# The last block's LayerNorm, split between two phases of a convolution and RWKV-7 block

## The chip, the cores and the metric

The kernel runs on one core of one Trainium2 chip. The metric is the device time of one execution in microseconds (us); several runs are given, with their median. The profile is of one further execution.

## The reference

One decoder block for 2048 tokens of width 1024, in float32. One input projection feeds two branches; both end in a projection of their own, are merged by gates, go through an output projection and are added to the residual. A final RMSNorm closes it.

```python
def _conv_branch(val, gate, og, conv_k, conv_b, ln_g, ln_b, w_o):
    u = val * jax.nn.sigmoid(gate)
    u = _causal_depthwise_conv(u, conv_k, conv_b)      # width 31
    u = _layernorm(u, ln_g, ln_b, LN_EPS)              # over the 1024 channels
    u = jax.nn.silu(u) * jax.nn.silu(og)
    return u @ w_o
```

The other branch is RWKV-7 time mixing: r, k, v, a decay and a learning rate from low-rank (LORA) projections, a delta-rule recurrence over 16 heads, a norm per head, times a gate, times `w_o` of its own. In short: x is normed and modulated, projected to all of these; out = RMSNorm(x + gate · (merged branches @ `w_out`)).

## The kernel before

**Tiling.** Channels lie on the 128 partitions, so 1024 channels are 8 tiles, and the tokens go in 4 blocks `b` of 512: a tile is 128x512, 256 KB. A projection of one output tile (`project`) is 24 matmuls of 128x128 by 128x512: 8 input tiles, each three times, since a float32 is split into a high and a low part (hi·hi, lo·hi, hi·lo). The weights' two parts are made once, stored (`kh_in`, `kl_in`, `kh_ro`, `kl_ro`, `kh_o`, `kl_o`) and loaded as `w_hi` and `w_lo`; `presplit` makes them for the two out projections, as side work.

**Phase 1** runs over the blocks, and in a block over four groups `g` of four heads. A group is one call of `slot`: it emits the projections of its two pairs of heads (k, r, vv each) and between them "fill" projections (convolution gate and value, and four gates). `order(b, g)` lists them: after the first pair's three come `FIRST` = 5 fills, after the second pair's the rest. At the head of a block but the first stands the LORA projection; the input tiles of the next block are loaded as `hf` and split to `h_hi` and `h_lo` when four items of the last slot are left (`rest == 4`); in the last block those are the tiles of `z_d` of block 0, which phase 2's first projections need, and which phase 1 already emits at its end.

Everything else is written as generators (`pair`, `group`, `taps`, `lnorm_first`, `sides`, ...), which a planner polls while the program is written. Each step waits until the planner's own count of time says that its operands, buffers or an engine are free, and is emitted there. So the order on each engine is fixed when the program is written, and on the chip an instruction waits only for semaphores. All of SP's DMA issues stand in one queue. Shared 128x512 buffers are handed out by a ring `hx` of `HXB` = 7. The four `As` buffers of two groups and the two `uv` buffers are allocated in `opened` at the head of a slot, which waits until the group before the last has been normed.

A group's path: `pair` loads `wf` (its slice of the LORA weights), makes `wl`, `As` matrices and so on; `group` inverts the small triangular systems with transfers through DRAM (`dA`, `La`, `dT`, back to `As`), transposes `Tn`, goes over the chunks, and stores the normed outputs times gate (`zb`, `zr` loaded, `z_d` stored).

**Convolution and its LayerNorm.** `taps` makes a tile by 31 operations on DVE and stores it in `y_d`. `lnorm_first(b)` has three passes over the 8 tiles. Pass 1 loads and sums them (7 additions), and a matmul with ones gives the mean. Pass 2 loads again, subtracts, squares and sums; a matmul and a few steps give `rl`, the reciprocal standard deviation. Pass 3 loads again, and per tile: times `rl`, tanh and affine form on ACT, (tanh + 1) times it, times the gate tile from `co_d`, stored in `u_d`. For blocks 0 to 2 this runs on POOL one block later. For block 3 it runs on DVE at the end of phase 1 (`last_norm`), with buffers from `more`, to which `lend(3)` lends three of `hx`.

**Phase 2** is written per block without the planner, and a scheduler orders it: `cproj` (for b > 0), then `pout` (x + merged @ `w_out`, four column blocks of 96 matmuls 128x256), `addx`, the final RMSNorm `finish` (8 DVE operations `xt<-xt,rs,fg`, 8 stores `out<-xt`), and `rproj(b + 1)`. The loads `zt<-z_d` and `zt<-u_d` (`lsplit`) feed these with 8 buffers `ld`. Two facts matter here. The tiles `xt{n}` (residual rows) and `mr{n}` (merged sums of the next block) share a buffer, tag `mr{n}`, so `rproj`'s first write of `mr` waits for the store `out<-xt` of the same n. And its PSUM tiles `ps_main` have two buffers.

The profile gives line 132 for every operation, since a helper records them all; operations are told apart by their names, without numbers.

Of the kernel before, what the change touches and what calls it, by code (L numbers as in the profile page):

```python
# [9 lines left out]
F32 = mybir.dt.float32  # L10
# [34 lines left out]
LDB = 8  # L45
SLACK = 2.0
KEPT = ("in",)
FILL = ("c", "1", "3", "4", "2", "c", "1", "3", "4", "2")
LAST = ("c0 10 20 c1 21 11 22 c2 23", "c3 12 24 c4 25 13 26 c5 27", "c6 14 30 c7 31 15 32 33 34 35",
        "16 36 37 40 41 17 42 43 44 45 46 47")  # L50
DMA_RATE = 330e3
FIRST = 5
AHEAD = 0.7
BANKS = {"aux": 2, "late": 1, "xo": 2}
# [20 lines left out]
def hybrid_block(ctx: ExitStack, tc: tile.TileContext, x, vecs, convk, w2a2, final_g, ada, w_in, w_co, w_ro, w_o, crow, out,  # L75
# [199 lines left out]

    u_dram = scratch("u_d")

    grow_d = dp.tile([D], F32, name="grow_d", tag="grow_d")
# [243 lines left out]

    hx = Ring(HXB, hx0)
    t2r = Ring(T2B, lambda name: e2.tile([P, TB], F32, name=name, tag="t2", bufs=T2B))
    wr = Ring(WB, lambda name: whl.tile([P, KT, P], F32R, name=name, tag="w", bufs=WB))
# [251 lines left out]
    def pair(G, q_, box):  # L777
        b, pr, uv, Asb = G.b, 2 * G.g + q_, G.uv, G.As[q_]
        wf = e1.tile([P, 2, P], F32, name="wf", tag="wf")
# [35 lines left out]
        k = box["k"]  # L815
        yield ok(k)
        KR = l3.tile([P, NCH // 2, 4 * CH], F32, name="KR", tag="KR", bufs=KRB)
        BK = l3.tile([P, NCH // 2, 4 * CH], F32, name="BK", tag="BK", bufs=BKB)
# [73 lines left out]
        nc.scalar.copy(rk, pb)  # L892
        yield when(lambda: "v" in box)
        vv = box["v"]
# [13 lines left out]
    def opened(b, g, h, lora):  # L908
        G = Group()
        G.b, G.g, G.h, G.lora, G.tri, G.pairs, G.chained, G.gated, G.normed = b, g, h, lora, 0, 0, False, False, False  # L910
        G.uv = l3.tile([P, NCH, 2, P], F32, name="uv", tag="uv", bufs=2)
        G.dN = dp.tile([2, 2, NCH // 2, 2, 2, 32], F32, name="dN", tag="dN", bufs=3)
        G.As = [l3.tile([P, 2, NCH, P], F32, name="As", tag="As", bufs=ASB) for _ in range(2)]
        G.R = [{}, {}]
        return G
# [4 lines left out]
    def group(G, before):  # L920
        g, b, As, uv, R = G.g, G.b, G.As, G.uv, G.R
        yield when(lambda: G.tri == 2)
# [4 lines left out]
        for q in range(2):  # L927
            for e in range(2):
                p0 = 64 - 64 * e
                for bk in range(2):  # L930
                    sl = slice(p0 + 32 * bk, p0 + 32 * bk + 32)
                    nc.sync.dma_start(dA[q, :, :, e, bk].rearrange("h c s t -> s (h c) t"), heads(As[q])[sl, e::2, sl])
        La = lt.tile([P, 32, 32], F32, name="La", tag="La", bufs=1)
        dAl = dA.rearrange("q h c e k s t -> (q h c e k) s t")
# [31 lines left out]
        for q in range(2):  # L966
            for e in range(2):
# [4 lines left out]
                yield idle("SP", 0.1)  # L972
        yield when(lambda: G.pairs == 2 and (before is None or before.chained))
        yield ok(*As)

# [78 lines left out]
        locked[0] = False  # L1054
        O = uv[:, 0::2]
# [133 lines left out]

    convs = []  # L1190

    def taps(b, j, u, before):
        if before is not None:
            yield when(lambda: before.done)
        yield ok(u)
        yj = e2.tile([P, TB], F32, name="yj", tag="yj", bufs=1)
        acc = pc.tile([P, TB], F32, name="acc", tag="acc")
        nc.vector.tensor_scalar(out=acc, in0=u[:, HALO:], scalar1=ck[:, j, HALO:HALO + 1], scalar2=vc("conv_b", j),
                                op0=ALU.mult, op1=ALU.add)
        for i in range(HALO):  # L1200
            yield idle("DVE", AHEAD)
            nc.vector.scalar_tensor_tensor(out=acc if i + 1 < HALO else yj, in0=u[:, i:i + TB],
                                           scalar=ck[:, j, i:i + 1], in1=acc, op0=ALU.mult, op1=ALU.add)
        yield ok(yj)
        nc.sync.dma_start(y_dram[b][j], yj)
# [4 lines left out]

    def lnorm_first(b, hx):

# [7 lines left out]
        eng = nc.vector if b + 1 == NB else nc.gpsimd  # L1220
        yield hx.room(3, 1)
        ys, nxt = yload(0), yload(1)
        for j in range(1, KT):
            yj = nxt
            if j + 1 < KT:
                yield hx.room(1, 1)
                nxt = yload(j + 1)
            yield ok(ys, yj)
            eng.tensor_tensor(out=ys, in0=ys, in1=yj, op=ALU.add)
            hx.give(yj)  # L1230
        yield burst(ok(ys), free, bank("late"))
# [33 lines left out]
        hx.give(qs, rt, mean)  # L1265
        def both_of(j):
            yj, ct = yload(j), hx.take("lnc")
            nc.sync.dma_start(ct, co_dram[b][j])
            return yj, ct

        nxt = None
        for j in range(KT):
            if nxt is None:
                yield hx.room(3, 1)
                nxt = both_of(j)
            else:
                yield hx.room(1)
            yj, ct = nxt
            th, nxt = hx.take("lnth"), None
            if j + 1 < KT and b + 1 == NB and hx.room(2)() is not None:  # L1280
                nxt = both_of(j + 1)
            yield ok(yj, rl)
# [79 lines left out]
    def sides(b, g):  # L1362
        if b + 1 < NB:
            yield from xnorm(b + 1, XN[g])
            if g == 1:
                normed[0] = b + 1
        if b == 1 and g == 0:
            yield from gate_col()
        if b and g == (0 if b + 1 == NB else 1):
            yield from lnorm_first(b - 1, hx)  # L1370
            if b + 1 == NB:
                yield from lend(3)
        if b:
            for _ in range(0 if b + 1 == NB else (1, 1, 3, 3)[g]):
                n_ = later.pop(0)
                for half in range(2):
                    yield from presplit(*n_, half)
# [19 lines left out]
    def last_norm():  # L1397
        yield when(lambda: len(convs) == KT * NB and convs[-1].done)
        yield from lnorm_first(NB - 1, more)

# [13 lines left out]
    def order(b, g):  # L1414
# [11 lines left out]
        for q in range(2):  # L1426
            for name, t_ in (("k", T_K), ("r", T_R), ("vv", T_V)):
                yield name, q, t_ + 2 * g + q
            yield from fill(FIRST if q == 0 else len(todo))

# [15 lines left out]
    def slot(b, g, h, lora, new):  # L1446
        until(lambda: not Gs[:-1] or Gs[-2].normed)
        G = opened(b, g, h, lora)
# [123 lines left out]
    def lsplit(src, hl=None):  # L1572
# [3 lines left out]
        return hi, lo  # L1576

    def cproj(b, uhl, mhl):
        for n in range(KT):
# [40 lines left out]
    for b in range(NB):  # L1620
# [115 lines left out]
```

## Time and profile before

| | |
|---|---|
| three runs | 2885.52, 2889.28, 2889.45 us; median 2889.28 us |
| the profiled execution | 2893.26 us, its span 2891.5 us |
| TensorE's mean granted clock | 0.984 |
| TensorE (PE) busy | 2722.4 us, 94% |
| VectorE (DVE) busy | 2067.5 us, 72% |
| ScalarE (ACT) busy | 1092.9 us, 38% |
| GpSimd (POOL) busy | 1195.6 us, 41% |
| phase 1 ends at about | 2420 us |

A row of the timeline gives start, duration, engine, operation, output and inputs; a bracket behind it gives how long the engine had stood idle and what ended that. "SPq" is a DMA issue on SP's queue: its duration is that of issuing, not of the transfer. In the chain of waits each piece is released by the piece above it. In the table by stage a number in brackets counts instructions, and the granted clock is a share of full speed.

### The profile page before, as it was taken

To read this page: it belongs to the slowest core of one execution; us is meant where nothing else is said; L and a number is where in the kernel's file an instruction comes from. 1 tells how busy PE (TensorE), PEld (TensorE's weight loads), DVE (VectorE), ACT (ScalarE), POOL (GpSimd) and SP (SyncE) were. 2 spreads that over 40 slices of the span, in tenths; PEclk is the share of its full clock that TensorE was granted. 3 is DMA by queue.
4 is the path that set the end of the run, shared out by engine and by line. 5 is a ranking of instruction groups with operands and counts; after the bars stand their busy time and mean duration, and the time that the engine had idled before them with its cause. 6 is when DMAs were issued, how large, how long until landed. Compare 5 with 4: busy or idle time off the path is not lost. (4 is left out here: it accounts for less than half of the span.)

```text
span 2891.5 us, 52406 instructions
## 1 busy us (share of the span) xinstructions
PE 2722.4 (94%) x19472; PEld 2195.2 (76%) x19472; DVE 2067.5 (72%) x3598; ACT 1092.9 (38%) x2181; POOL 1195.6 (41%) x1725
## 2 busy tenths in 40 slices
PE   6999999989999999999999998999999998999998
PEld 5777777767777777777777776877777777898988
DVE  6877887869677878886878786888887576343343
ACT  5545444434243434443434343324343334121211
POOL 1564746533528364534564553474543612000000
PEclk9999999989999999999999999999999999999999
DMA  8776867666758677767666776676665778777664
GB/s 329 258 286 206 292 218 265 236 233 228 235 185 290 199 255 242 275 222 238 231 251 223 249 255 197 220 269 215 227 230 191 273 247 315 259 239 247 215 226 175
DMA packets 370959, 697.26 MB, mean 241 GB/s; under 512 B 135184, under 2 KB 153936, under 8 KB 370704
## 3 DMA queue, kind: packets, MB, share of 16 engines
q1 hardware_dynamic: 370704, 693.91, 70.3%
q8 instruction: 154, 2.52, 0.4%
q14 instruction: 101, 0.83, 0.1%
HBM read 500.63 MB, written 192.02 MB: 240 GB/s over the span
## 5 line engine op out<-in xcount | busy, mean ns | idle before, releaser
L132 PE MATMUL ps_main<-h_hi,w_hi 128*128 128x512 f32 x2432 | 1016.3, 418 | 16.7 <-DVE lora L132 4.6
L132 PE MATMUL ps_main<-h_hi,w_lo 128*128 128x512 f32 x2432 | 966.9, 398 | 25.3 <-POOL w_lo L132 14.6
L132 PE MATMUL ps_main<-h_lo,w_hi 128*128 128x512 f32 x2432 | 961.3, 395 | 0.5 <-DVE h_lo L132 0.5
L132 DVE SCALAR_TENSOR_TENSOR acc<-u,ck,acc 128x512 f32<-128x512 f32 x928 | 698.0, 752 | 27.9 <-POOL u L132 2.2
L132 PEld LDWEIGHTS ps_main<-h_hi,w_lo 128*128 128x128 f32 x2432 | 462.2, 190 | 140.1 <-POOL w_lo L132 18.7
L132 PEld LDWEIGHTS ps_main<-h_hi,w_hi 128*128 128x128 f32 x2432 | 463.3, 190 | 128.4 <-issue 13.3
L132 PEld LDWEIGHTS ps_main<-h_lo,w_hi 128*128 128x128 f32 x2432 | 463.7, 191 | 96.3 <-issue 8.7
L132 POOL TENSOR_TENSOR w_lo<-w_st,w_hi 128x1024 fp32r<-128x1024 f32 (+1 forms) x82 | 165.0, 2012 | 332.5 <-ACT w_hi L132 288.5
L132 ACT ACTIVATE th<-ps_main 128x512 f32<-128x512 f32 x160 | 95.5, 597 | 360.2 <-PE ps_main L132 311.5
L132 POOL TENSOR_TENSOR TT<-TT,itmp 128x126 f32<-128x126 f32 (+22 forms) x496 | 209.5, 422 | 38.9
L132 POOL TENSOR_TENSOR itmp<-La,TT 128x126 f32<-128x126 f32 (+22 forms) x496 | 203.5, 410 | 37.7 <-issue 7.9
L132 ACT CAST w_hi<-w_st 128x1024 fp32r<-128x1024 f32 (+1 forms) x135 | 127.4, 945 | 221.6 <-DMA w_st<-w_co_t 78.4
L132 DVE SCALAR_TENSOR_TENSOR S<-xo,pe,Se 64x64 f32<-64x64 f32 x512 | 145.0, 283 | 91.9 <-PE xo L132 69.4
L132 ACT COPY uv<-xo 64x256 f32<-64x256 f32 (+1 forms) x192 | 81.2, 439 | 251.3 <-PE xo L132 184.7
L132 DVE TENSOR_TENSOR w_lo<-w_st,w_hi 128x1024 fp32r<-128x1024 f32 x53 | 74.5, 1405 | 68.3 <-PE ps_main L132 51.6
L132 DVE TENSOR_TENSOR As<-aux,maskA 128x512 f32<-128x512 f32 x128 | 82.3, 685 | 49.0 <-PE aux L132 48.9
L132 ACT ACTIVATE Se<-S,pe 128x128 f32<-128x128 f32 x256 | 89.0, 397 | 67.2 <-DVE S L132 66.7
L132 PEld LDWEIGHTS aux<-KR,BK 64*128 64x128 f32 x1024 | 66.3, 191 | 44.3 <-POOL KR L132 21.1
L132 PE MATMUL aux<-KR,BK 64*128 64x128 f32 x1024 | 80.0, 290 | 20.7 <-POOL KR L132 14.0
L132 POOL TENSOR_TENSOR wlo<-wf,wl 64x128 fp32r<-64x128 f32 x64 | 31.3, 489 | 159.2 <-ACT wl L132 156.7
L132 DVE TENSOR_TENSOR xt<-pout,xt 128x256 f32<-128x256 f32 x64 | 24.4, 420 | 100.1 <-PE pout L132 100.1
L132 PEld LDWEIGHTS xo<-S,KR 128*128 128x128 f32 x512 | 77.1, 189 | 20.7 <-ACT Se L132 4.3
(283 smaller groups left out, 5005.4 us busy)
## 6 DMA issues: line engine op xcount, KB each, us to landing
w_hi<-kh_in SPq DMA_DIRECT2D x219, 512.0 KB
w_lo<-kl_in SPq DMA_DIRECT2D x219, 512.0 KB
w_st<-w_in_t SPq DMA_DIRECT2D x73, 512.0 KB
kh_in<-w_hi SPq DMA_DIRECT2D x71, 512.0 KB
kl_in<-w_lo SPq DMA_DIRECT2D x71, 512.0 KB
lny<-y_d SPq DMA_DIRECT2D x96, 256.0 KB
w_hi<-kh_ro SPq DMA_DIRECT2D x32, 512.0 KB
w_lo<-kl_ro SPq DMA_DIRECT2D x32, 512.0 KB
```

Of the source, the lines that this page charges most:

```text
L132: r = f(*a, **k)
```

## The change

1. Block 3's y tiles are summed by `taps` as each is finished, in an `hx` buffer `ysum`; `lnorm_first` takes the sum and leaves pass 1 out. Behind `rl` it stores `rl` to DRAM (`rl_d`) and ends. Pass 3 is done in phase 2, by `ulast`, which takes the place of `lsplit(u_dram[3])`: 17 loads (`rl`, eight `yt`, eight `ct`) instead of eight, three DVE and two ACT operations a tile ahead of the split.
2. The weight splits of `presplit` in blocks 1, 2, 3 go by `LATE_W`, 6, 6 and 4, where before 8 and 8 stood in blocks 1 and 2 and none in 3. `LEND` is 1 instead of 3. Pass 3 of blocks 0 to 2 loses its early loads (they were for block 3 alone).
3. `As` is taken in `pair`, when the group before the last has been chained, `uv` when it has been normed; the wait at the head of `slot` goes. `group` waits for `before.merged` ahead of its `La` load.
4. In the last group of block 3 the second pair's projections come after 1 fill instead of 5 (`FIRST_LAST`), and the loads of `z_d` of block 0 begin when 9 items are left, not 4 (`HLAST`).

```diff
+LEND = 1
+LATE_W = ((), (1, 1, 2, 2), (1, 1, 2, 2), (1, 1, 1, 1))
+FIRST_LAST = 1
+HLAST = 9
...
     def pair(G, q_, box):
-        b, pr, uv, Asb = G.b, 2 * G.g + q_, G.uv, G.As[q_]
+        b, pr = G.b, 2 * G.g + q_
...
+        yield when(lambda: G.prior is None or G.prior.chained)
+        Asb = l3.tile([P, 2, NCH, P], F32, name="As", tag="As", bufs=ASB)
+        G.As.append(Asb)
...
-        yield when(lambda: "v" in box)
+        yield when(lambda: "v" in box and (G.prior is None or G.prior.normed))
+        if q_ == 0:
+            G.uv = l3.tile([P, NCH, 2, P], F32, name="uv", tag="uv", bufs=2)
...
     def group(G, before):
+        yield when(lambda: before is None or before.merged)
         La = lt.tile([P, 32, 32], F32, name="La", tag="La", bufs=1)
...
     def taps(b, j, u, before):
+        if b + 1 == NB and j == 0:
+            yield hx.room(1)
+            ysum.append(hx.take("ysum"))
+            nc.scalar.copy(ysum[0], yj)
+        elif b + 1 == NB:
+            yield ok(ysum[0], yj)
+            nc.vector.tensor_tensor(out=ysum[0], in0=ysum[0], in1=yj, op=ALU.add)
...
-    def lnorm_first(b, hx):
+    def lnorm_first(b, hx, ys=None):
...
+        if b + 1 == NB:
+            yield ok(rl)
+            nc.sync.dma_start(rl_d, rl)
+            hx.give(rl)
+            return
...
-                yield from lend(3)
+                yield from lend(LEND)
...
-            for _ in range(0 if b + 1 == NB else (1, 1, 3, 3)[g]):
+            for _ in range(LATE_W[b][g]):
...
-            yield from fill(FIRST if q == 0 else len(todo))
+            yield from fill(len(todo) if q else FIRST_LAST if (b, g) == (NB - 1, 3) else FIRST)
...
     def slot(b, g, h, lora, new):
-        until(lambda: not Gs[:-1] or Gs[-2].normed)
...
-            if new is not None and rest == 4:
+            if new is not None and rest == (4 if b + 1 < NB else HLAST):
...
+    def ulast(hl):
+        rl = f2.tile([P, TB], F32, name="rl", tag="rl", bufs=1)
+        nc.sync.dma_start(rl, rl_d)
+        for j in range(KT):
+            yt, ct = ldt("yt", y_dram[NB - 1][j]), ldt("ct", co_dram[NB - 1][j])
+            th = ob.tile([P, TB], F32, name="uth", tag="uth")
+            nc.vector.tensor_tensor(out=yt, in0=yt, in1=rl, op=ALU.mult)
+            nc.scalar.activation(th, yt, AF.Tanh, scale=hlg[:, j:j + 1], bias=hlb[:, j:j + 1])
+            nc.scalar.activation(yt, yt, AF.Identity, scale=vc("conv_ln_g", j), bias=vc("conv_ln_b", j))
+            nc.vector.scalar_tensor_tensor(out=yt, in0=th, scalar=1.0, in1=yt, op0=ALU.add, op1=ALU.mult)
+            nc.vector.tensor_tensor(out=yt, in0=yt, in1=ct, op=ALU.mult)
+            split(hl[0][j], hl[1][j], yt, nc.vector)
+        return hl
...
-            uhl = lsplit(u_dram[b + 1], utiles())
+            uhl = lsplit(u_dram[b + 1], utiles()) if b + 2 < NB else ulast(utiles())
```

The first place at which the order changes is DVE's, in phase 2, between the output projection of block 1 and `rproj` of block 2 (`m_lo` is the split of block 3's z tiles, `vs`, `rs` and `rs_t` are the small steps of the final RMSNorm, `xt<-xt,rs,fg` its first big one). Before, from the last residual addition on:

```order
L132 TENSOR_TENSOR xt_26727<-pout,xt_26727 128x256
L132 TENSOR_TENSOR m_lo_27920<-zt,m_hi_27912 128x512
L132 TENSOR_TENSOR m_lo_27921<-zt,m_hi_27913 128x512
L132 TENSOR_TENSOR m_lo_27922<-zt,m_hi_27914 128x512
L132 TENSOR_REDUCE vs<-sq_26777 128x4
L132 TENSOR_SCALAR vs<-vs 128x4
```

Ten further small steps follow, and then the first `xt<-xt,rs,fg`. After, at the end of the same stretch of DVE's order, behind seven operations of the new third pass (`yt`) that stand between the last residual addition and these rows:

```order
L136 SCALAR_TENSOR_TENSOR yt_28356<-uth_28360,yt_28356 128x512
L136 SCALAR_TENSOR_TENSOR rs_t_27188<-rs_t_27188,vs_27184 128x4
L136 TENSOR_TENSOR yt_28356<-yt_28356,ct_28358 128x512
L136 SCALAR_TENSOR_TENSOR rs2_27187<-rs_t_27188,rs2_27187 128x4
L136 SCALAR_TENSOR_TENSOR yt_28368<-uth_28372,yt_28368 128x512
L136 TENSOR_TENSOR rs_t_27188<-rs2_27187 128x4
L136 TENSOR_TENSOR yt_28368<-yt_28368,ct_28370 128x512
L136 SCALAR_TENSOR_TENSOR rs_t_27188<-rs_t_27188,vs_27184 128x4
L136 TENSOR_TENSOR yt_28380<-yt_28380,rl_28330 128x512
L136 SCALAR_TENSOR_TENSOR rs2_27187<-rs_t_27188,rs2_27187 128x4
L136 SCALAR_TENSOR_TENSOR xt0_26613<-xt0_26613,rs2_27187,fg_25433 128x512
```

In all 13 `yt` operations stand ahead of the first `xt<-xt,rs,fg` that stood behind it before, one of them ahead of the last residual addition; the last is the multiplication of the fifth tile, `yt_28380`. SP's order at the same place, after:

```order
L136 DMA w_hi_27321<-kh_ro3_11786 128x1024
L136 DMA w_lo_27322<-kl_ro3_11787 128x1024
L136 DMA yt_28380<-y_d3_4_191 128x512
L136 DMA ct_28382<-co_d3_4_223 128x512
L136 DMA yt_28392<-y_d3_5_192 128x512
L136 DMA w_hi_27353<-kh_ro4_11981 128x1024
L136 DMA w_lo_27354<-kl_ro4_11982 128x1024
L136 DMA ct_28394<-co_d3_5_224 128x512
L136 DMA out<-xt0_26613 128x512
```

The load of the fifth y tile stands behind the weights of `ro` tile 3, and the weights of tile 4 now stand ahead of the stores `out`; before, six of these stores stood between the weights of tiles 3 and 4.

The second place is SP's queue at the end of block 2 (`hf<-xT3` are block 3's input tiles, `gc_d2_7` is the last gate of block 2, `zb` and `zr` are loaded for a pair's outputs). Before, all eight `hf` loads stand ahead of the weights `kh_in48`, some of the last of the block. After, three do, and the rest stand here:

```order
L136 DMA gc_d2_7_250<-th_18302 128x512
L136 DMA zb_18333<-bv_d2_4_119 128x512
L136 DMA zr_18334<-ro_d2_4_151 128x512
L136 DMA hf_18346<-xT3_66 128x512
L136 DMA hf_18359<-xT3_66 128x512
L136 DMA kh_o1_0_17936<-w_hi_18120 128x512
L136 DMA hf_18372<-xT3_66 128x512
L136 DMA kl_o1_0_17937<-w_lo_18121 128x512
L136 DMA hf_18392<-xT3_66 128x512
L136 DMA hf_18394<-xT3_66 128x512
```

They moved behind the last store of block 2 and among a `presplit`'s stores (`kh_o`, `kl_o`). At the start of block 2, `wf` of the first pair now stands ahead of four of the eight `As` loads that stood ahead of it before; and at the end of block 3, five of the eight loads of `z_d` of block 0 stand well ahead, where before four did.

More of the change, by code (lines that the diff above doesn't have):

```diff
@@ L276, in hybrid_block @@
     u_dram = scratch("u_d")
+    rl_d = dp.tile([P, TB], F32, name="rl_d", tag="rl_d")
     grow_d = dp.tile([D], F32, name="grow_d", tag="grow_d")
@@ L523, in hybrid_block @@
     hx = Ring(HXB, hx0)
+    hx1 = hx
     t2r = Ring(T2B, lambda name: e2.tile([P, TB], F32, name=name, tag="t2", bufs=T2B))
@@ L892, in pair @@
         nc.scalar.copy(rk, pb)
-        yield when(lambda: "v" in box)
+        yield when(lambda: "v" in box and (G.prior is None or G.prior.normed))
+        if q_ == 0:
+            G.uv = l3.tile([P, NCH, 2, P], F32, name="uv", tag="uv", bufs=2)
+        uv = G.uv
         vv = box["v"]
@@ L910, in opened @@
         G.b, G.g, G.h, G.lora, G.tri, G.pairs, G.chained, G.gated, G.normed = b, g, h, lora, 0, 0, False, False, False
-        G.uv = l3.tile([P, NCH, 2, P], F32, name="uv", tag="uv", bufs=2)
+        G.merged = False
+        G.prior, G.uv, G.As = Gs[-2] if len(Gs) > 1 else None, None, []
         G.dN = dp.tile([2, 2, NCH // 2, 2, 2, 32], F32, name="dN", tag="dN", bufs=3)
-        G.As = [l3.tile([P, 2, NCH, P], F32, name="As", tag="As", bufs=ASB) for _ in range(2)]
         G.R = [{}, {}]
@@ L920, in group @@
     def group(G, before):
-        g, b, As, uv, R = G.g, G.b, G.As, G.uv, G.R
+        g, b, As, R = G.g, G.b, G.As, G.R
         yield when(lambda: G.tri == 2)
@@ L973, in group @@
         yield when(lambda: G.pairs == 2 and (before is None or before.chained))
+        uv = G.uv
         yield ok(*As)
@@ L1053, in group @@
                     cp(As[q][prow(e), :, e::2, rcol(e)], pg[e].rearrange("p c (h n) -> p h c n", h=2)[prow(e ^ q)])
-        locked[0] = False
+        locked[0], G.merged = False, True
         O = uv[:, 0::2]
@@ L1188, in conv @@
         evac(value(project(h, ("in", T_VAL + j)), convs[-3:-2]))
-    convs = []
+    convs, ysum = [], []
     def taps(b, j, u, before):
@@ L1220, in lnorm_first @@
         eng = nc.vector if b + 1 == NB else nc.gpsimd
[L1221 to L1230, printed above, removed]
+        if ys is None:
+            yield hx.room(3, 1)
+            ys, nxt = yload(0), yload(1)
+            for j in range(1, KT):
+                yj = nxt
+                if j + 1 < KT:
+                    yield hx.room(1, 1)
+                    nxt = yload(j + 1)
+                yield ok(ys, yj)
+                eng.tensor_tensor(out=ys, in0=ys, in1=yj, op=ALU.add)
+                hx.give(yj)
         yield burst(ok(ys), free, bank("late"))
@@ L1264, in lnorm_first @@
                 yield idle("DVE", 0.3)
-        hx.give(qs, rt, mean)
-        def both_of(j):
-            yj, ct = yload(j), hx.take("lnc")
-            nc.sync.dma_start(ct, co_dram[b][j])
[L1269 to L1281, printed above, removed]
+        hx.give(qs, rt)
+        hx1.give(mean)
+        if b + 1 == NB:
[4 more added lines that the diff above has]
+        for j in range(KT):
+            yield hx.room(3, 1)
+            yj, ct, th = yload(j), hx.take("lnc"), hx.take("lnth")
+            nc.sync.dma_start(ct, co_dram[b][j])
             yield ok(yj, rl)
@@ L1398, in last_norm @@
         yield when(lambda: len(convs) == KT * NB and convs[-1].done)
-        yield from lnorm_first(NB - 1, more)
+        yield from lnorm_first(NB - 1, more, ysum[0])
     def proj(h, ti, name, box):
@@ L1576, in lsplit @@
         return hi, lo
+    def ulast(hl):
+        rl = f2.tile([P, TB], F32, name="rl", tag="rl", bufs=1)
+        nc.sync.dma_start(rl, rl_d)
+        for j in range(KT):
+            yt, ct = ldt("yt", y_dram[NB - 1][j]), ldt("ct", co_dram[NB - 1][j])
[7 more added lines that the diff above has]
+        return hl
     def cproj(b, uhl, mhl):
```

## The prediction

> **What bounds the kernel now.** I read the page first, then the same counters cut by stage, then the chain of waits and the timeline where TensorE stands still. The page says who is busy:
>
> ```profile
> span 2891.5 us, 52406 instructions
> PE 2722.4 (94%) x19472; PEld 2195.2 (76%) x19472; DVE 2067.5 (72%) x3598; ACT 1092.9 (38%) x2181; POOL 1195.6 (41%) x1725
> ```
>
> TensorE is busy in 94% of the span, and the change adds no projection and removes none. So nothing it does can be worth more than TensorE's waits, about 2891.5 − 2722.4 = 169 us, and an edit counts only where it makes or closes one of them. The table by stage (stretch, length, busy time of PE, PEld, DVE, ACT and POOL with counts, granted clock, DMA share, GB/s) says where they are:
>
> ```profile
> 1160.00:2290.00 1130.00, 1077.59 (x8144) 851.08 (x8144) 881.57 (x1514) 441.12 (x896) 573.61 (x869) 0.99 0.69 232
> 2290.00:2420.00 130.00, 119.65 (x902) 94.46 (x900) 95.41 (x152) 46.86 (x80) 45.47 (x50) 0.99 0.76 263
> 2420.00:2475.00 55.00, 46.56 (x383) 45.29 (x383) 23.93 (x44) 23.48 (x58) 0.00 (x0) 0.94 0.93 345
> 2475.00:2892.00 417.00, 400.52 (x2308) 353.68 (x2307) 162.34 (x314) 79.85 (x175) 0.00 (x0) 0.99 0.66 225
> ```
>
> The table begins at 1160 us, since up to there the two programs give TensorE the same order. Blocks 1 (from its second half) to 3 lose 1130.00 − 1077.59 = 52 us in many small pieces. The last group of block 3, where the old third pass stands, loses 130.00 − 119.65 = 10.4 us. The change of phase loses 55.00 − 46.56 = 8.4 us, and the rest of phase 2 16.5 us. A stall has a second price, which the same table shows over short stretches:
>
> ```profile
> 1763.00:1773.00 10.00, 8.70 (x127) 7.05 (x127) 7.33 (x13) 2.39 (x4) 2.76 (x3) 0.66 0.65 233
> 2306.00:2311.00 5.00, 4.77 (x16) 3.77 (x16) 3.03 (x5) 3.29 (x6) 3.06 (x6) 0.66 0.55 208
> 2622.00:2632.00 10.00, 7.51 (x33) 5.84 (x33) 1.43 (x3) 0.00 (x0) 0.00 (x0) 1.00 0.98 374
> ```
>
> The ten microseconds from 1763 had a clock of 0.66: at half speed for 6.8 us, since 10 × 0.34 = 3.4 lost and half speed loses half of its time. The five from 2306 lost 5 × 0.34 = 1.7. The stall at 2622 cost no clock at all. These are the stalls in front of them (start, duration and operation of the first matmul after the stall; in brackets the wait and its releaser):
>
> ```profile
> 1194.73 0.80 PE L132 MATMUL aux<-lw,wl 128*128 128x512 f32 x1 [2.73 <-ACT wl L132]
> 1764.14 0.23 PE L132 MATMUL late<-Tn,As 32*32 32x32 f32 x1 [3.26 <-DVE Tn L132]
> 2305.64 0.50 PE L132 MATMUL ps_main<-h_hi,w_hi 128*128 128x512 f32 x1 [2.79 <-ACT h_hi L132]
> 2365.99 0.45 PE L132 MATMUL xo<-uv,tk 128*64 128x64 f32 x8 [2.05 <-DVE uv L132]
> 2625.41 0.50 PE L132 MATMUL ps_main<-o_hi,w_hi 128*128 128x512 f32 x1 [2.49 <-DVE mr L132]
> ```
>
> So a stall over 2.7 us was followed by up to 3.4 us of lost clock, and one of 2.49 us by none. The Trainium skill, page "TensorE: Matmul & The Clock Gate", section "What's actually happening", says that the clock falls to half only after a whole idle window of about 3.4 us. The 2.79 us stall with 0.66 behind it speaks against that as a strict rule, and the measurement decides; by the page, the stalls that are removed below would give back some 3 us less and the sum would be that much higher.
>
> **Step 1: the third pass moves into phase 2, onto the boundary of blocks 1 and 2 (+11 us).** That boundary is the one place in phase 2 where TensorE waits for a chain of DVE, DMA and DVE. The chain that ended last, over 2605 to 2627:
>
> ```profile
> 2616.66 1.35 DVE xt L132 x2
> 2618.01 6.52 DMA out<-xt
> ...
> 2624.66 0.70 DVE mr L132
> ...
> 2625.41 1.65 PE ps_main L132 x6
> ```
>
> Read it backwards. TensorE's second projection needs a PSUM buffer (there are two), which `mr` must empty. `mr` writes into the buffer of an `xt` tile, so it waits until `out<-xt` has been stored, 6.52 us. The store waits for the final RMSNorm's first operation on DVE. The order shown above puts 13 operations of 128x512 of the new third pass ahead of that operation: five multiplications by `rl`, four of the tanh form, four by `ct`. They cost what such an operation costs in phase 2:
>
> ```profile
> L132 DVE SCALAR_TENSOR_TENSOR mr<-rth,ps_main 128x512 f32<-128x512 f32 x24 | 16.3, 686 | 64.7 <-PE ps_main L132 38.1 <-DMA rth<-gr_d 20.2 <-DMA out<-xt 6.3
> ```
>
> 13 × 0.686 = 8.9 us, of which one lies before the last residual addition: 8.2 us at most stay. The loads set a second bound. The last of the 13 needs the fifth y tile, and SP issues that behind the weights of the fourth `ro` tile:
>
> ```profile
> 2612.52 2.80 SPq L132 DMA_DIRECT2D zt<-u_d  x4
> 2617.12 0.32 SPq L132 DMA_DIRECT2D w_hi<-kh_ro  x1
> 2617.53 0.38 SPq L132 DMA_DIRECT2D w_lo<-kl_ro  x1
> ...
> 2471.29 4.99 DMA zt<-u_d
> ```
>
> Those two issues end at 2617.91, since they wait for TensorE to release weight buffers. A load of the same size took 4.99 us in the chain at the boundary before. 2617.9 + 0.3 + 5.0 + 0.7 for the multiplication and 0.2 for the last small step is 2624.1, against 2616.66: 7.4 us later. Everything behind keeps its distance, so the stall of 2.49 grows to about 10 us. It is then far over 2.79, and I add the 3.4 us of lost clock: +10.8, taken as **+11**. Low end: the load comes in 3 us and no clock is lost, +5. High end: the load takes the 6.52 us of the store and the weights ahead of `out` wait too, +14. The ACT operations and splits that come with it stand behind `mr`, and DVE is busy for 162 of 417 us there.
>
> **Step 2: the loads of block 3's input (+3 us).** Before, the eight `hf` loads from xT were issued by 1720.6, ahead of the last tile of block 2. Now five of them stand behind the store of the last `gc` tile and a pair's `zb` and `zr`. In the rows of before that store is the one at 1726.49, and one `zb` and `zr` follow it:
>
> ```profile
> 1719.65 0.96 SPq L132 DMA_DIRECT2D hf<-xT  x2
> ...
> 1726.49 0.32 SPq L132 DMA_DIRECT2D gc_d<-th  x1
> ...
> 1728.13 0.32 SPq L132 DMA_DIRECT2D zr<-ro_d  x1
> ```
>
> The first row of the LORA projection on TensorE:
>
> ```profile
> 1730.41 0.39 PE L132 MATMUL ps_main<-h_hi,w_hi 128*128 128x512 f32 x1
> ```
>
> The cast to `h_hi`, and the late wait for `hf` that step 3 needs, on ACT:
>
> ```profile
> 1725.34 0.62 ACT L132 CAST h_hi<-hf 128x512 fp32r<-128x512 f32 x1 [6.86 <-PE ps_main L132]
> ...
> 2304.97 2.67 ACT L132 CAST h_hi<-hf 128x512 fp32r<-128x512 f32 x4 [6.45 <-DMA hf<-z_d]
> ```
>
> So they start at about 1728.5; with two weight stores between them the last is issued at about 1732. It lands at 1737 with the 4.99 us from above and its cast and split take 1.3 us (0.62, and 0.69 as above). The LORA projection starts at 1730.41 and can use three of eight tiles, 2 us of matmuls: a stall of about 6 us and 3.4 us of clock, +9.4. In return the work of the last group, which runs on POOL and SP whether or not TensorE stands, gets these 9 us, so that the stall of 3.26 us at 1764.14 and the 3.4 us of clock behind it go: −6.7. Net **+3**, between −1 (the loads are issued early because their buffers were free) and +10 (the later stall stays).
>
> **Step 3: the end of phase 1 (−5 us).** The third pass leaves DVE there:
>
> ```profile
> L132 DVE SCALAR_TENSOR_TENSOR lny<-lnth,lny 128x512 f32<-128x512 f32 x8 | 9.4, 1173 | 0.6 <-ACT lny L132 0.4
> L132 DVE TENSOR_TENSOR lny<-lny,lnr 128x512 f32<-128x512 f32 x8 | 8.7, 1094 | 0.1
> L132 DVE TENSOR_TENSOR lny<-lny,lnc 128x512 f32<-128x512 f32 x8 | 7.6, 954 | 0.0
> ```
>
> 25.7 us of DVE and sixteen loads go, but TensorE's whole loss in that stage is 10.4 us, and the largest piece (2.79 at 2305.64) waits for z tiles from HBM (6.45 on ACT, above). These loads begin earlier now (`HLAST`), five instead of four of them well ahead: −2 of the stall and −1 of its 1.7 us of clock. The 2.05 us at 2365.99 waits for DVE itself: −1. Small ones −1. Together **−5**, from −10 (all of it) to 0. The sums of y cost nothing: seven additions and a copy take the place of seven additions with eight loads, beside the 31 tap operations that each tile takes on the same engine.
>
> **Step 4: a pair takes its buffers later (−3 us).** At the start of block 2, from 1188.90, four `As` loads took 3.17 us of SP ahead of `wf`, from which `wl` is made, and TensorE waited 2.73 us for `wl`:
>
> ```profile
> 1188.90 3.17 SPq L132 DMA_DIRECT2D As<-dT  x4
> 1192.12 0.45 SPq L132 DMA_DIRECT2D wf<-w2a  x1
> ```
>
> `wf` now stands ahead of those four: −2.7 and −1.7 of clock. The same four loads come later, so the transposed `Tn` they feed does too, and I give back 1.5: **−3**, from −6 to 0.
>
> **Step 5: the rest.** The weight splits in 6, 6, 4 and the LayerNorm of block 2 on POOL move work between blocks whose POOL is half idle (574 of 1130 us). No row prices their shuffle of 52 us of small waits. I take 0, and −8 to +8, some 15% of these 52 us on either side.
>
> The sum is 11 + 3 − 5 − 3 + 0 = +6 us. The profiled execution took 2893.26 us, its span and 1.8 around it, so it would take 2899; it lies 4.0 above the median of 2889.28. On that median the forecast is **2895 us**.
>
> **The rivals.**
> - *Faster, about 2880.* Taking the third pass out closes the end of phase 1 altogether: 10.4 us of waits and 1.7 of clock, and 5 of the 8.4 at the change of phase with 3.3 of clock (55 × 0.06), in all −20; with step 4, −23; with steps 1 and 2 at +11 and +3, −9. For it: DVE is busy 95.41 of 130 us there, a quarter of that with the third pass. Against it: the longest stall there ends with z tiles from HBM, which the third pass does not hold up. It decides if TensorE loses under 3 us between 2290 and 2420.
> - *No change, about 2890.* The boundary waits, but DVE runs the 13 operations in its free time, and the loads come in 3 us: step 1 is +5 and the rest −5. For it: the stall of 2.49 us at this boundary cost no clock. Against it: the y load is behind `w_lo<-kl_ro` in any case.
> - *Much slower, about 2905.* Step 1 at +14 and step 2 at +9 with the stall at 1764 still there, −5 −3: +15. For it: every stall over 2.7 us before was followed by lost clock. Against it: group work does not need TensorE in that time.
> - *The change does not do what it says:* the scheduler keeps the third pass away from the boundary. The order denies it, so this has 2 in 100.
>
> **How the numbers follow.** The forecast (2890 to 2901) has 0.40, of which 0.30 lies above 2895; faster 0.25; no change 0.15; much slower 0.18; the last 0.02. About 0.2% (5.8 us) is what a measurement of this kernel can tell from no change. Slower by over that is 0.30 + 0.18 = 0.48, within it 0.10 + 0.15 + 0.02 = 0.27, faster 0.25. The range goes to 2878, below the faster rival, and to 2910, above the much slower one; about 2 in 10 lie beyond, for the unknown of step 5.
>
> **What would show it.** Step 1: a PE stall of about 10 us ended by `mr` near 2630, with a clock near 0.66 behind it. Step 2: a PE stall at the LORA projection of block 3 that `h_hi` or `h_lo` ends. Step 3: the stage with the last group loses 5 us instead of 10.4. Step 4: no wait for `wl` at the start of block 2. The forecast is wrong if the first finishing operation still starts within 2 us of the last residual addition plus the small steps, or if blocks 1 to 3 gain or lose over 10 us in small waits that no step names.

## The result and the profile after

The changed kernel takes 2892.59 us (median of 20 runs, 2887.07 to 2900.46), the kernel before 2888.86 us (20 runs): a ratio of 1.0013, 95% interval 1.0002 to 1.0025. It is slower by 3.7 us, by a little less than the 0.2% that the forecast called slower. One execution of the kernels below, in experiment 5, took 6732.45 us (the other eleven 2872.32 to 2889.38); its ratio leaves it out, and the cause is open. The profiled execution has a span of 2895.8 us. The table by stage of the changed kernel, with the same columns and the same first stretches as before:

```profile
1160.00:2290.00 1130.00, 1075.01 (x8124) 849.82 (x8123) 879.69 (x1513) 439.66 (x894) 576.78 (x882) 0.98 0.70 231
2290.00:2420.00 130.00, 124.67 (x941) 100.31 (x940) 75.56 (x135) 40.35 (x73) 41.84 (x38) 0.99 0.67 227
2420.00:2475.00 55.00, 49.49 (x389) 47.77 (x389) 25.00 (x55) 22.01 (x58) 0.00 (x0) 0.94 0.95 352
2475.00:2896.00 421.00, 398.00 (x2283) 351.33 (x2282) 171.75 (x321) 89.91 (x184) 0.00 (x0) 0.98 0.66 224
```

DVE's load in the last group fell from 95.41 to 75.56 us and TensorE's loss there from 10.4 to 5.3 us; phase 2 loses 23.0 us where it lost 16.5. A table by clock time mixes stages when one kernel runs ahead, so I also compared equal work: the projections and output projections are 9984 matmuls in either kernel. Below they are called main matmuls and counted from 0 in the order in which they start; the time from one of them to a later one is the time of a piece of work. Here are these times in us for all traces of this study (worked out from the traces; the columns are the boundary of blocks 1 and 2, block 2 up to the last tile, the boundary of blocks 2 and 3, block 3, the end of phase 1 with the change of phase, and in phase 2 the boundary of blocks 1 and 2):

```
matmul                        3504   3600   5160   5328   6864          8400
                             -3600  -5160  -5328  -6864  -7440         -8640
before                        43.9  497.2   62.8  494.2  159.6          52.7
before, second trace          41.9  499.1   60.2  502.8  160.0          54.1
after                         39.1  500.4   64.4  498.8  150.3          62.3
finish_first                  41.0  502.0   63.0  501.2  152.0          56.3
no_third_math                 38.0  501.2   62.9  501.3  149.2          56.7
hf_early                      37.7  499.4   46.8  500.7  154.7          62.6
finish_first_hf_early         38.7  501.1   47.9  500.9  156.9          56.8
old_weight_splits             37.7  495.2   51.8  492.5  159.1          62.3
old_last_order                38.7  497.7   61.6  500.1  154.7          62.5
old_buffers                   42.6  503.8   58.8  505.0  150.8          63.1
third_pass_alone              43.6  502.6   48.4  489.9  154.5          61.5
finish_first_old_splits       36.8  496.3   49.8  497.9  159.2          56.0
  "  _hf_early                37.6  493.5   53.7  491.9  158.1          54.4
```

Against the first trace of before, the change is −4.8, +3.2, +1.6, +4.6, −9.3 and +9.6 us in these columns. The second trace says how far to trust one of them: equal programs differ by 0.4 to 2.6 us in most, by 8.6 in block 3.

The boundary in phase 2 is the clearest. The chain of waits that ended last over 2590 to 2640, changed kernel:

```profile
2608.41 5.27 DMA yt<-y_d
...
2613.71 0.70 DVE yt L136
...
2616.84 0.82 ACT yt L136
...
2619.89 5.39 DVE xt L136 x8
2625.28 1.00 DVE yt L136 x2
...
2626.40 0.69 DVE mr L136
...
2627.14 13.08 PE ps_main L136 x44
```

Before, the path into the first `xt` was the split of a z tile and twelve small steps; now it is a load of a y tile, the multiplication by `rl`, two tanh and two affine operations on ACT, and the last of the 13 operations on DVE. TensorE's row, and the table over that stretch (clock third from the right):

```profile
2627.14 0.80 PE L136 MATMUL ps_main<-o_hi,w_hi 128*128 128x512 f32 x1 [9.41 <-DVE mr L136]
```

```profile
2622.00:2634.00 12.00, 6.86 (x18) 5.45 (x19) 8.27 (x13) 2.19 (x3) 0.00 (x0) 0.57 0.84 297
```

The stall is 9.41 us where it was 2.49, and the clock behind it is halved. In the first trace of before it stayed at 1.00 there. In the second trace of before (experiment 9) a stall of 2.39 us at the same matmul was followed by 0.66:

```profile
2629.95 0.79 PE L132 MATMUL ps_main<-o_hi,w_hi 128*128 128x512 f32 x1 [2.39 <-DVE mr L132]
```

```profile
2629.00:2634.00 5.00, 4.05 (x11) 3.24 (x12) 1.37 (x2) 0.00 (x0) 0.00 (x0) 0.66 1.05 413
```

So the boundary costs 9.6 us against the first trace and 8.2 against the second. At the boundary of blocks 2 and 3 in phase 1 the late loads are seen on SP and on TensorE:

```profile
1725.26 1.74 SPq L136 DMA_DIRECT2D hf<-xT  x2
1727.14 0.34 SPq L136 DMA_DIRECT2D kh_o<-w_hi  x1
1729.59 0.32 SPq L136 DMA_DIRECT2D hf<-xT  x1
1729.96 0.42 SPq L136 DMA_DIRECT2D kl_o<-w_lo  x1
1734.29 0.79 SPq L136 DMA_DIRECT2D hf<-xT  x2
```

```profile
1732.88 0.49 PE L136 MATMUL ps_main<-h_hi,w_hi 128*128 128x512 f32 x1 [1.83 <-ACT h_hi L136]
1734.32 0.51 PE L136 MATMUL ps_main<-h_lo,w_hi 128*128 128x512 f32 x1 [0.94 <-DVE h_lo L136]
...
1738.28 0.80 PE L136 MATMUL ps_main<-h_hi,w_hi 128*128 128x512 f32 x1 [0.83 <-ACT h_hi L136]
```

```profile
1728.00:1740.00 12.00, 8.40 (x28) 5.39 (x27) 4.71 (x7) 3.90 (x7) 11.22 (x17) 0.81 0.81 274
```

Between the weight split's store and the last two `hf` issues SP waited for 3.9 us. The waits of SP's queue between 1723 and 1736 (us in total, times, longest) say for what:

```profile
SPq L136 <- DVE h_lo L136: 2.9, 2, 2.0
SPq L136 <- POOL w_lo L136: 2.0, 1, 2.0
```

All three are waits of `hf` issues: two for earlier input tiles to be split, one for the weight split's own operation on POOL. Input tiles and weight splits share the buffers of the ring `hx`. At the start of block 2 `wf` is issued ahead of the six `As` loads, and no wait for `wl` is left in that stretch; a wait of 1.66 us for `Tn`, at 1198.89, is new there:

```profile
1188.67 0.41 SPq L136 DMA_DIRECT2D wf<-w2a  x1
...
1190.21 3.55 SPq L136 DMA_DIRECT2D As<-dT  x6
```

### The profile page after: what moved, and what is told of

It is laid out like the page before. It is cut to its first block, busy times and chain, and to the rows that moved or that the text cites. A ratio compares the mean times of both kernels' runs of the same rounds, so it can differ in the third digit from the quotient of the medians.

```text
span 2895.8 us, 52384 instructions
## 1 busy us (share of the span) xinstructions
PE 2722.7 (94%) x19472; PEld 2198.1 (76%) x19472; DVE 2056.5 (71%) x3597; ACT 1092.6 (38%) x2182; POOL 1195.3 (41%) x1726
## 5 line engine op out<-in xcount | busy, mean ns | idle before, releaser
L136 DVE TENSOR_TENSOR w_lo<-w_st,w_hi 128x1024 fp32r<-128x1024 f32 x52 | 72.5, 1393 | 68.0 <-PE ps_main L136 51.8
L136 ACT ACTIVATE t<-ps_main,mu 128x512 f32<-128x512 f32 x96 | 65.8, 686 | 73.1 <-PE ps_main L136 63.3
```

The source lines that it names most:

```text
L136: r = f(*a, **k)
```

## The experiments

Each ratio is to the kernel before, from runs on the same chip, with its 95% interval. In microseconds, 0.001 is 2.9. A difference of two ratios carries both intervals, some 0.002 or 5 to 7 us either way.

**1. The finishing operations first.** `rl` is loaded behind the RMSNorm of block 1:

```diff
     def ulast(hl):
-        rl = f2.tile([P, TB], F32, name="rl", tag="rl", bufs=1)
-        nc.sync.dma_start(rl, rl_d)
+        rl = rls[0]
...
             for tt in range(NTT):
                 finish(tt, rall)
+            if b == NB - 3:
+                rls.append(f2.tile([P, TB], F32, name="rl", tag="rl", bufs=1))
+                nc.vector.tensor_copy(rls[0][:, 0:1], xts[-1][-1][:, 0:1])
+                nc.sync.dma_start(rls[0], rl_d)
```

> The changed kernel with one edit: rl is loaded behind a one-column DVE copy that reads the last tile of the final RMSNorm of block 1, so that no operation of the third pass can stand ahead of that RMSNorm on DVE. Nothing else moves. Theory (the 13 third-pass operations ahead of the first finishing operation, with the loads and ACT operations that they wait for, make the boundary's stall of 9.41 us and its half clock): the stall falls back to 2 to 3 us with the clock at 1.00 behind it, the boundary gives back the 9.7 us that it cost, and the time is 2883 us, ratio 0.998 to before. Rival (it is SP's queue: 16 loads instead of 8 and the weights of tile 4 ahead of the stores): the loads are all still there, the stall stays over 6 us and the time over 2889 us.

Measured: 2887.64 us, ratio 0.9991 (0.9977 to 1.0005), 0.0022 or 6.4 us under the changed kernel. DVE and TensorE at the boundary:

```profile
2620.02 5.39 DVE L136 SCALAR_TENSOR_TENSOR xt<-xt,rs,fg 128x512 f32<-128x512 f32 x8
2625.44 0.15 DVE L136 COPY rl<-xt 128x1 f32<-128x1 f32 x1
2629.18 0.69 DVE L136 SCALAR_TENSOR_TENSOR mr<-rth,ps_main 128x512 f32<-128x512 f32 x1 [3.58 <-DMA out<-xt]
```

```profile
2629.92 0.79 PE L136 MATMUL ps_main<-o_hi,w_hi 128*128 128x512 f32 x1 [3.65 <-DVE mr L136]
```

The store in the chain of waits:

```profile
2621.36 7.72 DMA out<-xt
```

`mr` waits for the store again, as before the change, but 3.58 us instead of 2.61: it starts 9.2 us behind the first `xt` (2629.18 and 2620.02) where that took 8.0 (2624.66 and 2616.66). The store is issued as soon behind the first `xt` as before (1.34 and 1.35 us), but takes 7.72 us where it took 6.52 and, in the second trace, 6.43. The stall is 3.65 us, and the clock behind it is 0.68 over ten us, so 3.6 of the 9.6 us are left. Both theories hold a part: the operations made 6 us of it, and the rest is a store that takes longer, with lost clock behind it.

**2. No arithmetic in the third pass, all loads kept.**

```diff
-            nc.vector.tensor_tensor(out=yt, in0=yt, in1=rl, op=ALU.mult)
-            nc.scalar.activation(th, yt, AF.Tanh, scale=hlg[:, j:j + 1], bias=hlb[:, j:j + 1])
-            nc.scalar.activation(yt, yt, AF.Identity, scale=vc("conv_ln_g", j), bias=vc("conv_ln_b", j))
-            nc.vector.scalar_tensor_tensor(out=yt, in0=th, scalar=1.0, in1=yt, op0=ALU.add, op1=ALU.mult)
-            nc.vector.tensor_tensor(out=yt, in0=yt, in1=ct, op=ALU.mult)
+            nc.vector.tensor_tensor(out=yt[:, 0:1], in0=rl[:, 0:1], in1=ct[:, 0:1], op=ALU.mult)
```

> The changed kernel, which leaves out the arithmetic of the last block's third pass: per tile one operation on one column that reads rl and the co tile, and the split. All 17 loads stay. Theory (DVE order): the stall at the boundary is 2 to 3 us, the time 2883 us as with the finishing operations first. Rival (loads on SP): the stall stays over 6 us and the time over 2889 us. If this is faster by over 2 us than the kernel with the finishing operations first, the third pass costs something in its new place too.

Measured: 2888.08 us, ratio 0.9998 (0.9982 to 1.0014), which by time alone is not told apart from the changed kernel; the boundary takes 56.7 us as with the finishing operations first (56.3), with this stall:

```profile
2620.93 0.80 PE L136 MATMUL ps_main<-o_hi,w_hi 128*128 128x512 f32 x1 [4.06 <-DVE mr L136]
```

So the third pass costs nothing that these runs could show in its new place once it stands behind the finish (the rest of phase 2, from matmul 8640 on, takes 222.2 to 222.4 us in every trace), and the 2 to 4 us that are left are not from DVE's work. What both kernels share against before is 17 loads for eight, which may be what slows the store; no run here takes loads away, so that is not shown.

**3. Block 3's input earlier,** and **4. both edits:**

```diff
-            if new is not None and rest == (4 if b + 1 < NB else HLAST):
+            if new is not None and rest == (HB3 if b + 2 == NB else 4 if b + 1 < NB else HLAST):
```

with `HB3 = 6`.

> The changed kernel with the loads of block 3's input begun 6 items ahead of the end of block 2 instead of 4. Its order on SP then has all eight ahead of the last gate's store. Theory (step 2: five late loads make waits of 1.83, 0.94 and 0.83 us and half clock, 7.4 us by the places of equal matmuls, and hide the Tn stall that follows, 5.4 us): the waits at the LORA projection go, the Tn stall of over 3 us at about 1764 comes back, and the time stays within 3 us of the changed kernel, 2890 us. Rival (the late loads are a pure loss): the time falls by 7 us to 2885.

> Both edits: the finishing operations first at the boundary and block 3's input loaded from 6 items ahead. If the two places are independent the gains add: 2883 us with the 0 to -3 us of the early loads, 2880 to 2884 us. If the early loads are a pure gain, 2876 us.

Measured: 2884.73 us, ratio 0.9980 (0.9966 to 0.9994), and for both 2879.21 us, 0.9954 (0.9938 to 0.9970). The early loads are worth 9.5 us by ratio; the stretch over the boundary of blocks 2 and 3 fell from 64.4 to 46.8 us. The Tn stall did not come back, and the time is the rival's. But the edit moved more than the loads: the Tn matmul stands 21 main matmuls later in that order (behind matmul 5304, not 5283), which gives the group the time. Its data came no earlier: the second transpose into `Tn` ends 23.4 us behind matmul 5208, and in the changed kernel the matmul that waits for it starts 18.9 us behind matmul 5208. So the later place took the stall away, and whether the late loads had hidden it, as my theory said, is not settled by this run. Not all of the 17.6 us reach the end: at the end of phase 1 both kernels with early loads take 4 to 5 us more (154.7 against 150.3, 156.9 against 152.0). The gains of 1 and 3 add: 6.4 + 9.5 = 15.9, measured 17.

**5. The weight splits of before:**

```diff
-LATE_W = ((), (1, 1, 2, 2), (1, 1, 2, 2), (1, 1, 1, 1))
+LATE_W = ((), (1, 1, 3, 3), (1, 1, 3, 3), (0, 0, 0, 0))
```

> The changed kernel with the weight splits of before: 8 items in block 1, 8 in block 2, none in block 3. Theory (the four items that moved into block 3 make its 4.5 us of extra waits, and the ring buffers that a split holds at the end of block 2 make the late input loads): block 3 gives back 4 us, two of the five late loads stand early again and give back 3 us, the time is 2885 to 2886 us. Rival (the splits cost nothing wherever they stand, as the prediction took): within 2 us of the changed kernel, 2891 to 2895 us.

Measured: 2879.95 us, ratio 0.9968 (0.9948 to 0.9988): 0.0045 or 13 us under the changed kernel, twice what I expected. The table of equal work says where: 12.6 us at the boundary of blocks 2 and 3, 6.3 in block 3, 5.2 in block 2; at the end of phase 1 it loses 8.8, because the last z tiles are now loaded late (the cast to `h_hi` waited 12.28 us for `hf<-z_d`):

```profile
2288.50 0.80 PE L136 MATMUL ps_main<-h_hi,w_hi 128*128 128x512 f32 x1 [8.76 <-ACT h_hi L136]
```

One trace of block 2 or 3 can scatter by as much as is read here, but all traces together say the same: the seven with the new splits take 500.8 us in block 2 and 501.1 in block 3 on average, the six with the old ones 497.3 and 494.9.

**6. The last group's order of before:** `FIRST_LAST = 5`, `HLAST = 4`.

> The changed kernel with FIRST_LAST 5 and HLAST 4 as before. Theory (of the 8.7 us that the end of phase 1 gained, about half is from the earlier z loads and the order of the last group, half from the third pass that left): 4 us of it go, 2896 to 2897 us. Rival (all of it is from the third pass): 2892 to 2893 us.

Measured: 2896.96 us, ratio 1.0033 (1.0014 to 1.0051), 5.8 us over the changed kernel by ratio, 4.4 by medians, and 4.4 us in the column of the end of phase 1. The difference of the two ratios, 0.0020, is no larger than their intervals; with the column, of one trace, it fits the theory and not the rival.

**7. The buffers taken at the head of a slot,** with the wait there:

```diff
-        yield when(lambda: G.prior is None or G.prior.chained)
-        Asb = l3.tile([P, 2, NCH, P], F32, name="As", tag="As", bufs=ASB)
...
-        yield when(lambda: before is None or before.merged)
...
+        until(lambda: not Gs[:-1] or Gs[-2].normed)
         G = opened(b, g, h, lora)
```

> The changed kernel with As and uv taken at the head of a slot and the wait there, as before. Theory (step 4: taking them in the pair removed the wait for wl and its half clock at the start of block 2): the wait of 2.7 us for wl and the 4.6 us come back, 2897 us. Rival (the later buffers let group work slip and make the 7.5 us of small waits in blocks 2 and 3 that no step named): the time falls by 3 us or more, to 2889 us or less.

Measured: 2902.49 us, ratio 1.0054 (1.0035 to 1.0073), 0.0041 or 12 us over the changed kernel: more than twice what I expected. The wait for `wl` is back,

```profile
1196.99 0.50 PE L136 MATMUL aux<-lw,wl 128*128 128x512 f32 x1 [2.99 <-ACT wl L136]
```

with 3.5 us in that column. Blocks 2 and 3 are longer too (503.8 and 505.0 against 500.4 and 498.8), by 3.4 and 6.2 us where equal programs differed by 1.9 and 8.6, and the boundary between them is shorter by 5.6; the profiled execution took 2910.43 us, 8 over the median. So where the rest of the 12 us arises is not shown.

**8. Part 1 alone:** experiment 7's edits, the old splits, `LEND = 3`, and the old order of the last group.

> Part 1 alone: the y sum and the third pass in phase 2, with the old weight splits, the old buffers, three lent buffers, and the old order of the last group. Theory: the boundary costs 9.7 us, the end of phase 1 gives back 4 to 5, all input loads of block 3 are early, nothing else moves much: 2893 to 2895 us. Rival (the part pays by itself, and it is the other parts that lose): 2886 us or less.

Measured: 2887.93 us, ratio 0.9996 (0.9977 to 1.0014), between the theory and the rival. The boundary in phase 2 costs its 9 us and the end of phase 1 gives back 5; the rest, 12 to 14 us in its trace, is the boundary of blocks 2 and 3 (48.4 us against 62.8 and 60.2).

**9. Before, a second trace.**

> The kernel before once more, for a second trace of it. If the Tn stall of 3.26 us at 1764 with its half clock and the 4.03 us behind it belong to that program, they are there again, and the stretch between the matmuls 5160 and 5328 takes 62.8 us again. If they were an accident of one execution, it takes 48 to 50 us, as in the kernels whose input loads are early.

Its profiled run took 2899.54 us. The two stalls are there again, and the stretch takes 60.2 us:

```profile
1758.62 0.18 PE L132 MATMUL late<-Tn,As 32*32 32x32 f32 x1 [3.40 <-DVE Tn L132]
...
1774.19 0.36 PE L132 MATMUL xo<-uv,As 64*64 64x64 f32 x1 [4.03 <-issue]
```

They belong to the program before. In part 1 alone the Tn matmul stands behind the same main matmul (5286) and finds its data in time: its `As` loads are issued from 1750.04, before from 1754.82, while TensorE is at the same place within half a microsecond. The group is 5 us ahead from the start of its inversion on (the first store `dA<-As` is issued at 1689.51, before at 1694.84). What made it so was not traced.

**10 and 11. The finishing operations first with the old splits,** without and with the early input.

> The changed kernel with the finishing operations first at the boundary and the weight splits of before. Alone the one gave 5 us and the other 13. If they are independent, the time is 2874 to 2876 us, ratio 0.995 to before; a rival in which the new splits only shifted the waits gives 2880 us as without the first edit.

> The same with block 3's input loaded from 6 items ahead as well. With the old splits five of the eight loads are early already, so little is left: theory 2872 to 2876 us, within 2 us of the run without; if the loads are the larger part of what the splits cost, as hf_early's 8 us say, and three late ones still cost half of it, 2870 us.

Measured: 2877.30 us, ratio 0.9949 (0.9927 to 0.9970), and 2873.52 us, ratio 0.9929 (0.9904 to 0.9955). Both beat both kernels; the last one has the lowest median of the study, 0.7% under before. The gains of 1 and 5 add (6.4 + 13 = 19.4, measured 18.5). The early loads lower the median by 3.8 us and the ratio by 0.0020, which is not clear of the two intervals; the stretch at that boundary does not show it (53.7 against 49.8), and the 6 us of block 3 are within what one trace can scatter.

## Why the prediction was right, and where it was not

The time, 2892.6 us, is in the range and 2.4 us from the forecast. The mechanisms of steps 1, 3 and 4 were there, and of step 2 the loss; the gain set against it is there too, but its reason stays open. That the sum holds is luck, because two errors cancel: steps 1 to 4 were to add 6 us and took 2.9 off against the first trace of before (9.6 + 1.6 − 9.3 − 4.8), and blocks 2 and 3 lost 7.8 us that no step had named. That is just inside the 10 us from which the forecast called itself wrong.

- **Step 1** said +11; the boundary measured +9.6 (+8.2 against the second trace), a stall of 9.41 us for about 10, half clock behind it. It was shown by taking the operations out of the way: 6 us went. The bound that I named was the fifth y tile's load. That was not it: DVE's multiplication of that tile came without a wait, and the chain went through the load of the third tile, which also stands behind weights on SP, and ACT's four operations, which I had put "behind `mr`". The first finishing operation came 8.4 us later (2619.89 against 2616.66, in a kernel 5.2 us ahead), where I said 7.4.
- **Step 2** said +3, made of +9.4 and −6.7; the equal work shows +7.9 up to matmul 5208 and −6.3 behind it, +1.6 together. The size is right. The reason for the second half stays open: experiment 3 took the late loads away and the Tn stall did not return, but its matmul stood later there. Loading early and the order that came with it were worth 17.6 us in that stretch of one trace (64.4 against 46.8; 7.4 of it up to matmul 5208, the rest behind it, where the edit also moved the group's work) and 9.5 in the whole by ratio; that before loses about as much there, by its two stalls, hid it.
- **Step 3** said −5; measured −9.3, near the end of its range. About half goes with the order of the last group and the earlier z loads (4.4 us in experiment 6's trace).
- **Step 4** said −3; measured −4.8 at its place (−2.8 against the second trace), with the later `Tn` for which I gave back 1.5 as a wait of 1.66 us. But the part is worth 12 us in the whole kernel (experiment 7), give or take 6; what I had not priced is not located.
- **Step 5**, "I take 0", failed. The weight splits in 6, 6, 4 cost 13 us, give or take 7: 12.6 us in experiment 5's trace at a place that step 2 had seen without tying it to the splits, and some 10 in blocks 2 and 3 by the averages given there, less the 8.8 us that they gain at the end of phase 1. A split's stores on SP stand among block 3's input loads, which wait for buffers and for the split itself, and with the old splits five of the eight loads go ahead of the last gate's store. My reason, that POOL is half idle, looked at the wrong resource.

Part 1 alone is −1 us, the splits +13, the buffers −12, the last order −6: −6 in all, measured +3.7. With the intervals of all four, that sum is uncertain by some 12 us, so it does not show whether the parts add. In the traces, at the boundary of blocks 2 and 3, they do not stand apart: 62.8 us before, 48.4 with part 1 alone, 64.4 with all four, 51.8 and 58.8 without the new splits and without the new buffers. That the Tn stall of before goes in some orders and not in others is accounted for in experiment 3 alone, by the later place of its matmul.

What a stall does to the clock has more rows now at one place, the boundary of blocks 0 and 1, where the instructions are equal: a stall of 2.91 us in the changed kernel with a clock of 1.00 behind it, and one of 3.97 us in experiment 1 with 0.68:

```profile
2483.00:2493.00 10.00, 9.00 (x40) 7.46 (x41) 2.02 (x3) 0.00 (x0) 0.00 (x0) 1.00 0.98 370
```

```profile
2489.00:2499.00 10.00, 8.97 (x28) 7.18 (x29) 2.05 (x3) 0.00 (x0) 0.00 (x0) 0.68 0.67 262
```

Taken alone, these two fit the rule of the whole idle window of about 3.4 us (the Trainium skill, page "TensorE: Matmul & The Clock Gate", section "What's actually happening"). The other traces do not. With the old order of the last group, a stall of 1.86 us at that matmul was followed by lost clock:

```profile
2475.43 0.50 PE L136 MATMUL ps_main<-m_hi,w_hi 128*128 128x512 f32 x1 [1.86 <-DVE mr L136]
```

```profile
2475.00:2480.00 5.00, 4.57 (x13) 3.63 (x14) 1.03 (x2) 0.00 (x0) 0.00 (x0) 0.66 1.05 411
```

Of the thirteen traces only two kept 1.00 there, the changed kernel's and the first one of before, with a stall of 2.84 us at 2489.19. So the prediction's sentence that every stall over 2.7 us before was followed by lost clock was not right, and the length of a stall alone does not tell what the clock does behind it. What else decides was not found.

## What to carry to other kernels

When work is moved to a later phase to relieve an engine, look up what it stands ahead of in that engine's order: the engine had time to spare there, but one short operation on it was what a store, and behind it a PSUM buffer, waited for. An edit that only shuffles side work is not free because its engine is half idle; ask which ring buffers and which queue positions it takes at the moment when the next block's loads must go out. And undo a many-part change part by part: here one part gained 12 us and another lost 13, and the sum hid both.

## What the runs showed of the hardware

Equal programs spread by 22 us (before: 2880.55 to 2902.30 in 20 runs), and the traces say where some of it arises: at the boundary of blocks 0 and 1 the same instructions gave stalls of 1.86 to 4.32 us, and the next 48 main matmuls took 11.0 us where the clock stayed at 1.00 and 12.6 to 13.9 where it was halved for a time. A store `out<-xt` of 256 KB took 6.43 and 6.52 us at the boundary of blocks 1 and 2 in the two traces of before, and 6.81 to 7.72 us in the five kernels with 17 loads there that have the third pass out of its way. The first 3504 main matmuls, the same in before and in nearly all kernels here, ended between 8.7 us earlier and 3.2 us later than in the first trace of before.
